# Where the summing transfers of two weight matrices run: moving them from the input projections to the GLA scan and the GLA up-projection

## The chip, the cores and the metric

The kernel runs on one core of one Trainium2 chip. The metric is the device time of one execution in microseconds (us), the median of several runs. A core has a matrix engine (TensorE, in the profile PE, with its weight loads as PEld), three engines for elementwise work (VectorE, in the profile DVE; ScalarE, ACT; GpSimd, POOL) and a queue engine (SyncE, SP). Each engine takes its instructions strictly in order from its own queue, and the five run beside one another, tied together by semaphores. Transfers (DMA) are issued as instructions of an engine's queue and then run on 16 DMA engines that all queues share.

## What is computed

One decoder block on 1024 tokens of width 1024, in float32. Cut to what bears on the change:

```python
proj = n @ w_in                       # split into z, xBC, dt, q, k, v, r, a1, g_ssd, g_gla
y_ssd = ssd_mixer(z, xBC, dt, ...)    # Mamba-2 branch: convolution, then a chunked scan
y_gla = gla_mixer(q, k, v, r, a1, ...)  # gated linear attention: a chunked scan
merged = sigmoid(g_ssd) * (y_ssd @ w_up_ssd) + sigmoid(g_gla) * (y_gla @ w_up_gla)
h = h + merged @ w_o                  # output projection of the mixer
q = rmsnorm(h) @ w_xq                 # query projection of the cross-attention
...                                   # attention over 256 memory tokens, then a SwiGLU FFN
```

## The kernel before

**Products.** Most large products are made by a Strassen scheme: the weight and the activation are cut into quadrants, and seven products of half the size (named B11, B21, T1, B22, T2, T3, T4) replace eight. That needs sums of quadrants. Each operand is then split into a high and a low float32r part, so that three fast passes stand for one float32 product; ScalarE makes the high part (tile `whi`, L233) and VectorE the low part (tile `wlo`, `split`, L228). A `Unit` (L285) makes 256 output columns in seven products of 12 matmuls of 128x512 each; its weight quadrants are in tile `raw`, and the sums of them (`left`, L304) are written to `sa` and `raw` by VectorE or GpSimd. Which of the two is chosen when the program is built: `either` (L85) asks a simple model of how long each of the two is already booked (`Meter`, L58). Everything that is called on GpSimd books time there, the issue of a transfer too, as if it were an elementwise operation over the transfer's whole size. The split weights go into rings of three buffers (L236), so VectorE and ScalarE can run at most some products ahead of TensorE.

**The sums of `w_o` and `w_xq`.** For these two matrices (class `Wide`, L1218) the four quadrant sums aren't made by the engines but by transfers in device memory: `weight_sums` (L482) issues, on GpSimd's queue, copies of quadrants into a buffer (`wos_d` for `w_o`, `xqs_d` for `w_xq`) and further transfers that add a second quadrant on the way (`accum_op`). With the adding ones cut in two halves, a matrix takes 12 transfers. Each is `pinned`: it stands in GpSimd's queue behind everything that was written before it for GpSimd. The FFN's `w_ffn_out` gets the same treatment in pieces (buffer `down_d`, L1821), whose adding transfers are not cut.

**Order of the work.** `run(main, (side, rate), ...)` (L448) walks through a main generator and takes `rate` steps of each side generator after each of its steps. The stages that matter here, in order:

- The z units (L895): 4 units, with `ssd_prep` and `gla_prep` as one side and `wsums`, the 24 summing transfers of both matrices in turn, as another at 0.36 transfers for each product.
- The xBC units (L1052): 6 units, beside them the convolution of the unit before (VectorE, tile `cv`), and again `wsums` at 0.36. Then `drain(wsums)` issues what is left.
- The SSD scan (L1066) beside the units for r, q, k and the first gates.
- The GLA scan (L1191): 5 gate units (35 products) as the main work, and `gla_steps` as the side. Each of the 8 chunks makes, among others, its output on TensorE, squares on ScalarE, a reciprocal root on GpSimd (tile `ss`, L217), a scaling on ScalarE (tile `o`, L1144) and transposes on TensorE (L55).
- The last gate unit, then the SSD up-projection `dense(0, ...)` and the GLA up-projection `dense(1, ...)` (L1366): 16 steps each, of 24 matmuls. A step of the second ends in `post_yg` (L1458): a gate, and then the sum of the two branches into tile `rq`, with the engine chosen by `either`. `wide_side` (L1472) prepares the first operands of the output projection beside it.
- The output projection `wo.steps()`, which reads `wos_d` and the `rq` tiles, then the query projection, which reads `xqs_d`, attention, and the FFN.

A scheduler places each engine's instructions in an order by priority and a model of time when the program is built; on the chip that order is fixed.

Of the kernel before, what the change touches and what calls it, by code (L numbers as in the profile page):

```python
# [16 lines left out]
P = 128  # L17
# [18 lines left out]
PRIO = 1000  # L36
# [42 lines left out]
def block_kernel(ctx: ExitStack, tc: tile.TileContext, t: dict, out: bass.AP):  # L79
# [3 lines left out]
    DVE, POOL = Meter(nc.vector, now, 0.06, 1.04e-3), Meter(nc.gpsimd, now, 0.08, 2.25e-3)  # L83

    def either(ap, slack=0.0):  # L85

        return POOL if POOL.after(ap) - slack < DVE.after(ap) else DVE
# [11 lines left out]
    def dram(name, *shape):  # L99
        return dr.tile(list(shape), F32, name=name, tag=name)  # L100
# [12 lines left out]
    gg_d = dram("gg_d", D, TOK)  # L113
# [4 lines left out]
    wos_d = dram("wos_d", 2 * D, HALF)  # L118
    xqs_d = dram("xqs_d", 2 * D, HALF)
# [10 lines left out]
    add = lambda e, o, a, b: e.tensor_tensor(o, a, b, ALU.add)  # L130
# [3 lines left out]
    pinned = tc.keep_in_program_order  # L134
# [289 lines left out]
    def group(units, B, then=(), nxt=None, frm=6, products=7, order=None):  # L424


        for u in units:
            u.load()
        then = list(then)
        many = len(units)  # L430
        for n, name in enumerate((order or (CHAIN if many > 1 else SPACED))[:products]):
            for x, u in enumerate(units):
                u.step(name, B)
                if many > 1:
                    B.upto((n + 1) * B.kh - (-(x + 1) * B.kh // many))
                if n == 6 and nxt:
                    nxt.upto((x + 1) * nxt.kh // many)
                if n >= frm and then:
                    then.pop(0).load()
                while len(posts) > lag[0]:  # L440
                    settle()
                    if n < 4:
                        break
                yield
        for u in then:
            u.load()

    def run(main, *rest, prio=0):  # L448

        owed = [0.0] * len(rest)  # L450
        for _ in main:
            for i, (g, rate) in enumerate(rest):
                owed[i] += rate
                while owed[i] >= 1.0:
                    owed[i] -= 1.0
                    with tc.high_priority(offset=prio):
                        next(g, None)
# [5 lines left out]
    def drain(g):  # L463
        for _ in g:
            pass

    def singles(units, B, then=()):

        for u, nxt in zip(units, list(units[1:]) + [None]):
            yield from group([u], B, [nxt] if nxt else then)  # L470
# [11 lines left out]
    def weight_sums(todo):  # L482


        jobs = []
        for A, d, n, k0 in todo:
            put = lambda m, d=d, n=n, k0=k0, kn=A.shape[2]: (
                d[(m * n + k0) * P:(m * n + k0 + kn) * P].rearrange("(k p) c -> p k c", p=P))
            q = {(i, j): A[j][:, :, half(i)] for i in range(2) for j in range(2)}
            jobs.append([(put(0), q[1, 0], 0), (put(2), q[0, 0], 0), (put(3), q[0, 1], 0), (put(0), q[1, 1], 1),  # L490
                         (put(2), q[1, 0], 1), (put(1), put(0), 0), (put(1), q[0, 0], 1), (put(3), put(1), 1)])
        for step in zip(*jobs):
            for o, a, more in step:
                kn = o.shape[1]
                for c in (slice(0, kn // 2), slice(kn // 2, kn)) if more and kn > 3 else (slice(0, kn),):
                    if more:
                        pinned(POOL.dma_start(o[:, c], a[:, c], accum_op=ALU.add))
                    else:
                        pinned(POOL.dma_start(o, a))
                    yield  # L500
# [72 lines left out]
    for k in range(NB):  # L573
        p = bank()
# [79 lines left out]
    B = Operands(hb, 4)  # L654
# [232 lines left out]
    xu = [Unit(w_in, 0, XBC0 + 256 * u) for u in XU]  # L887
    zu = w_in_units(Z0, 4, store_rows(sz_d))
    ru = w_in_units(R0, 4, store_rows(sr_d))
    qk = w_in_units(Q0, 2, store_rows(q_d)) + w_in_units(K0, 2, store_rows(k_d))  # L890
    gs = w_in_units(GS0, 4, store_rows(gs_d))
    gg = w_in_units(GG0, 4, store_rows(gg_d))
    prep = chain([ssd_prep(), gla_prep()])
    wsums = weight_sums([(t[w].rearrange("(j k p) c -> j p k c", j=2, p=P), d, 4, 0) for w, d in (("w_o", wos_d), ("w_xq", xqs_d))])
    run(singles(zu, B, xu[:1]), (prep, 1.0), (wsums, 0.36))  # L895
    drain(prep)
    settle_all()
    st2.close()
# [9 lines left out]
    class SSD:  # L908
# [69 lines left out]
        def gate(s):  # L978
            s.y = sp_.tile([P, 4, CH], F32, name="y", tag="y", bufs=3)
            for k in range(4):  # L980
                DVE.scalar_tensor_tensor(s.y[:, k], s.L[:, k], dcol[:, s.g * 4 + k:s.g * 4 + k + 1],
                                         s.py[:, k * P:(k + 1) * P], ALU.mult, ALU.add)
            mul(POOL, s.y, s.y, s.L[:, 4:8])
# [65 lines left out]
    cvp = pool("conv", 1, stack=st2)  # L1049
    pend = iter(())  # L1050
    for n, u in enumerate(XU):
        run(group([xu[n]], B, (xu + ru)[n + 1:n + 2]), (pend, 1.0), (wsums, 0.36))  # L1052
        drain(pend)
        pend = conv(u, xu[n])
        if n == 2:
            it[0].csb = sl_.tile([P, GH, CH], F32, name="xz", tag="xz", bufs=3)
            it[0].fetch_cs()
        if n == 4:
            it[0].load()
    drain(pend)  # L1060
    drain(wsums)
    st2.close()
    sp_ = pool("ssd", 1, stack=st3)
    ssd = ssd_steps()
# [92 lines left out]
    def gla_steps():  # L1157
        it = [GLA(c) for c in range(NCH)]
        it[0].load_qk()
        it[0].load()  # L1160
        it[1].load_qk()
        it[1].load()
        yield
        it[0].decay()
        it[0].start()
        yield
        it[0].attend()
        yield
        for i, a in enumerate(it):
            b = it[i + 1] if i + 1 < len(it) else None  # L1170
            c = it[i + 2] if i + 2 < len(it) else None
            a.out()
            yield
            if c:
                c.load_qk()
            a.scan()
            yield
            if b:
                b.decay()
                b.start()  # L1180
            yield
            a.norm()
            yield
            if b:
                b.attend()
            if c:
                c.load()
            yield

    gla = gla_steps()  # L1190
    run(singles(gs[2:] + gg[:3], B, gg[3:]), (gla, 8 * 5 / 30), prio=PRIO)  # L1191
    drain(gla)
    st4.close()
    st_early.close()

# [4 lines left out]
    ysg_d = dram("ysg_d", D, TOK)  # L1200
# [9 lines left out]
    def quad(src, base, i, j):  # L1210
        q = rp.tile([P, HALF], F32, name="ga", tag="ga")
        SP.dma_start(q, src[base + i * P:base + (i + 1) * P, half(j)])
        return q
# [152 lines left out]
    def dense(no, ins, post, pre=lambda o, j: None, js=JS, left=left):  # L1366

        todo = [(o, j) for o in range(NB) for j in (js if o + 1 < NB else js[::-1])]
        got = [pre(*x) for x in todo[:2]]
        for n, (o, j) in enumerate(todo):  # L1370
            w = left[NB * no + o]
            if n + 2 < len(todo):
                got.append(pre(*todo[n + 2]))
            cur = got[n]
            p = acc()
            m = 0
            for k in range(NB):
                for a, b in ((0, 0), (0, 1), (1, 0)):
                    PE.matmul(p, w[:, a, k], ins[k][:, b, half(j)], start=m == 0, stop=m == 3 * NB - 1)
                    m += 1  # L1380
            with ahead():
                post(o, j, p, cur)
            yield

    EVEN, ODD = ("op",) * 8, ("op",) * 6 + ("aux",) * 2
    i_ys, i_yg, i_q, i_xo = (paired(x) for x in (EVEN, ODD, EVEN, EVEN))
# [71 lines left out]
    def post_yg(o, j, p, gy):  # L1458
        g, y = gy
        gated(g, p)  # L1460
        q = wo.quad(o // 4, j)[:, o % 4]
        add(either(g), q, g, y)

    def post_wo(i, j, u, q):
        o = 4 * i + u
# [4 lines left out]
    wo = Wide(t["w_o"], wos_d, post_wo, ("aux",) * 7, ("m", "m", "m", "aux"), xT_d, 0.5)  # L1470

    def wide_side(x, n, m, pin=None):  # L1472
        for _ in range(n):
            yield
        x.load(1)
        for _ in range(m):
            yield
        x.load(2)
        yield
        x.prep(1, pin)  # L1480
        yield
        x.prep(2, pin)
        yield
# [18 lines left out]
            yield  # L1502

    run(dense(0, i_ys, post_ys, lambda o, j: gate(gs_d, o, j)), (fetch_gated(yg_d, sr_d, i_yg), 1.0))
    run(dense(1, i_yg, post_yg, lambda o, j: (gate(gg_d, o, j), quad(ysg_d, o * P, 0, j))), (wide_side(wo, 8, 4, pinned), 1.0))
    run(wo.steps(), (wide_side(xq, 7, 2), 1.0))


# [128 lines left out]
    for u in range(D_FF // 256):  # L1637
# [5 lines left out]
        gate = Unit(t["w_ffn_in"], 0, 256 * u, post=gpost, key="aux")  # L1643
# [38 lines left out]
    B = Operands(b_xo, 4, order=("B11", "T1", "B21", "B22", "T2", "T3", "T4"))  # L1682
# [139 lines left out]
    for u in range(1, len(gu)):  # L1822
        gate, up = gu[u]
# [78 lines left out]
```

## Time and profile before

| What | Value |
|---|---|
| Median of 3 runs | 1950.2 us (1948.35 to 1950.63) |
| The profiled execution's own time | 1951.16 us |
| Its span, first to last instruction | 1949.5 us |
| TensorE busy | 1901.7 us, 98% of the span |
| VectorE busy | 1352.9 us, 69% |
| ScalarE busy | 880.5 us, 45% |
| GpSimd busy | 509.4 us, 26% |
| Mean granted TensorE clock | 0.995 |
| Moved by GpSimd's transfers | 39.85 MB, 9.7% of the 16 DMA engines' time |

The page of the profile has the busy shares in 40 slices of the span (a digit is tenths). The view of windows gives, for stretches of the span, each engine's busy time with the number of its instructions, the granted TensorE clock, the DMA engines' mean busy share and the rate moved. TensorE's busy time alone says little, since matmuls overlap and their ends are modelled; the number of matmuls that a stretch holds says more. The view of waits gives, for each pair of a waiting group and its releaser, the sum, the number and the longest of the waits; "issue" as a releaser stands for a wait whose cause the profile doesn't name. The timeline gives start, duration, engine, line, operation, output and inputs, and in brackets the idle time of the engine before it.

### The profile page before, as it was taken

How to read it: one execution, taken by the hardware profiler on the slowest of the kernel's cores; microseconds unless marked ns; L12 is line 12 of the kernel's file. 1: busy time of each engine (PE TensorE's matmuls, PEld its weight loads, DVE VectorE, ACT ScalarE, POOL GpSimd, SP SyncE). 2: the span in 40 equal slices, each digit the busy share in tenths (PEclk: the TensorE clock that was granted, in tenths of full speed). 3: DMA queues.
4: the chain of work that ended last, by engine and by line, in shares of the span. 5: the costliest groups of instructions: out<-in, count | busy, mean ns of one | idle time of the engine just before them, and what ended most of it. 6: DMA issues, size and time to landing. Idle time of an engine off the chain costs nothing.

```text
span 1949.5 us, 26093 instructions
## 1 busy us (share of the span) xinstructions
PE 1901.7 (98%) x9680; PEld 1598.3 (82%) x9680; DVE 1352.9 (69%) x1949; ACT 880.5 (45%) x1521; POOL 509.4 (26%) x412
## 2 busy tenths in 40 slices
PE   7999989899999999999999999999999999999998
PEld 7998767778878888888888888888888888888888
DVE  7765858677767755553377786677878877766566
ACT  7534445455554344553235564543333333345243
POOL 0112444354544222000002100006444544330002
PEclk9999999999999999999999999999999999999999
DMA  9425698654654554595444430434665657387463
GB/s 345 139 93 187 194 282 249 151 184 152 186 179 137 193 157 153 210 374 172 140 151 157 157 98 12 146 103 128 172 180 149 166 154 191 87 298 267 158 225 122
DMA packets 242915, 341.04 MB, mean 175 GB/s; under 512 B 16458, under 2 KB 147764, under 8 KB 242788
## 3 DMA queue, kind: packets, MB, share of 16 engines
q1 hardware_dynamic: 225572, 293.23, 44.7%
q0 software_dynamic: 15488, 39.85, 9.7%
q10 hardware_dynamic: 1728, 6.29, 0.8%
q8 instruction: 76, 1.25, 0.3%
q14 instruction: 51, 0.42, 0.1%
HBM read 249.87 MB, written 129.30 MB: 195 GB/s over the span
## 4 chain that ended last, share of the span: by engine, by line
PE 84%; DVE 7%; issue 4%; POOL 2%; DMA 2%; ACT 1%; SPq 0%; POOLq 0%; DVEq 0%; ACTq 0%
PE acc L51 68%; PE bank L51 15%; PE bank L55 2%; DVE cv L73 2%; DVE wlo L73 2%; DVE hs L73 1%; DVE o L73 1%; DMA hl<-ys_d 0%; DMA down_d<-in_w_ffn_out_dram 0%; POOL ssum L73 0%; POOL raw L73 0%; DVE gx L73 0%; DMA raw<-in_w_ffn_in_dram 0%; DVE gy L73 0%; ACT cv L778 0%
## 5 line engine op out<-in xcount | busy, mean ns | idle before, releaser
L73 DVE TENSOR_TENSOR wlo<-raw,whi 128x512 fp32r<-128x512 f32 x272 | 237.6, 880 | 114.2 <-ACT whi L233 111.8
L233 ACT ACTIVATE whi<-raw 128x512 fp32r<-128x512 f32 x272 | 169.8, 631 | 260.6 <-PE acc L51 201.2
L51 PE MATMUL acc<-hl,wd 128*128 128x512 f32 x1152 | 263.8, 390 | 1.9 <-ACT wd L233 1.4
L51 PEld LDWEIGHTS acc<-hl,wd 128*128 128x128 f32 x1152 | 215.5, 188 | 48.5 <-ACT wd L233 2.6
L73 DVE TENSOR_TENSOR o<-acc,o 128x512 f32<-128x512 f32 x244 | 167.2, 685 | 89.6 <-PE acc L51 85.8
L51 PE MATMUL acc<-fs 128*128 128x512 f32 (+1 forms) x792 | 155.7, 355 | 0.1
L51 PEld LDWEIGHTS acc<-fs 128*128 128x128 f32 x792 | 130.7, 189 | 20.8 <-issue 0.5
L73 DVE TENSOR_TENSOR fs<-fr,fs 128x1024 fp32r<-128x1024 f32 (+1 forms) x78 | 93.0, 1226 | 36.7 <-ACT fs L233 36.5
L233 ACT ACTIVATE fs<-fr 128x1024 fp32r<-128x1024 f32 (+1 forms) x78 | 74.3, 984 | 93.7 <-PE acc L51 29.7
L73 POOL TENSOR_TENSOR ssum<-ssum,sq 128x512 f32<-128x512 f32 (+1 forms) x17 | 29.5, 1733 | 322.4 <-ACT sq L519 308.8
L233 ACT ACTIVATE whi<-sa 128x512 fp32r<-128x512 f32 x96 | 59.6, 627 | 102.5 <-PE acc L51 85.7
L73 POOL TENSOR_TENSOR sa<-raw 128x512 f32<-128x512 f32 x42 | 62.7, 1494 | 134.8 <-DMA raw<-in_w_in_dram 65.9
L73 DVE TENSOR_TENSOR wlo<-sa,whi 128x512 fp32r<-128x512 f32 x96 | 75.5, 787 | 23.9 <-ACT whi L233 23.0
L51 PE MATMUL acc<-ws 128*128 128x512 f32 x384 | 88.8, 389 | 0.0
L51 PEld LDWEIGHTS acc<-ws 128*128 128x128 f32 x384 | 72.0, 188 | 14.9
L73 POOL TENSOR_TENSOR raw<-raw,sa 128x512 f32<-128x512 f32 x34 | 47.8, 1406 | 138.0 <-DVE wlo L73 138.0
L51 PE MATMUL acc<-B22h,whi 128*128 128x512 f32 x192 | 76.9, 400 | 6.1 <-ACT whi L233 5.8
L51 PE MATMUL acc<-T2h,whi 128*128 128x512 f32 x192 | 76.8, 400 | 5.7 <-ACT whi L233 5.7
L51 PE MATMUL acc<-T4h,whi 128*128 128x512 f32 x192 | 76.4, 398 | 3.6 <-DVE o L73 3.5
L51 PE MATMUL acc<-B22h,wlo 128*128 128x512 f32 x192 | 76.6, 399 | 1.8 <-DVE wlo L73 1.7
L51 PE MATMUL acc<-T3h,wlo 128*128 128x512 f32 x192 | 75.4, 393 | 1.5 <-DVE wlo L73 1.5
L51 PE MATMUL acc<-T1h,whi 128*128 128x512 f32 x192 | 76.4, 398 | 0.1
(420 smaller groups left out, 4995.7 us busy)
## 6 DMA issues: line engine op xcount, KB each, us to landing
raw<-in_w_in_dram SPq DMA_DIRECT2D x26, 1024.0 KB, 7.1
raw<-in_w_ffn_in_dram SPq DMA_DIRECT2D x22, 1024.0 KB, 8.8
act_d<-o SPq DMA_DIRECT2D x77, 256.0 KB, 2.7
fr<-act_d SPq DMA_DIRECT2D x35, 512.0 KB, 5.4
down_d<-in_w_ffn_out_dram POOLq DMA_DIRECT2D x18, 768.0 KB, 7.3
fr<-down_d SPq DMA_DIRECT2D x20, 512.0 KB, 4.2
ga<-h_d SPq DMA_DIRECT2D x32, 256.0 KB, 6.8
csb<-cs_d SPq DMA_DIRECT2D x15, 512.0 KB, 3.9
```

Source lines behind the costliest of these rows:

```text
L51: return s.e.matmul(o, x, y, **kw)
L55: return s.e.transpose(o, x, i)
L73: return f(*a, **kw)
L233: pin(ACT.activation(hi, src, AF.Copy))
```

## The change

It does four things.

1. The summing transfers leave the z and xBC stages. Those of `w_o` now run beside the GLA scan, at 0.37 transfers for each product and at the scan's own raised priority, and what is left of them is issued after it; those of `w_xq` run beside the GLA up-projection, at 0.8 for each step.
2. The two matrices are no longer taken in turn: each has a sequence of its own.
3. The order within a sequence changes. It was: copy 0, copy 2, copy 3, add to 0, add to 2, copy 0 to 1, add to 1, add 1 to 3. Now copy 3 stands between "copy 0 to 1" and "add to 1". This holds for the FFN's pieces too.
4. The sum of the branches in `post_yg` always goes to GpSimd.

```diff
@@ weight_sums
-            jobs.append([(put(0), q[1, 0], 0), (put(2), q[0, 0], 0), (put(3), q[0, 1], 0), (put(0), q[1, 1], 1),
-                         (put(2), q[1, 0], 1), (put(1), put(0), 0), (put(1), q[0, 0], 1), (put(3), put(1), 1)])
+            jobs.append([(put(0), q[1, 0], 0), (put(2), q[0, 0], 0), (put(0), q[1, 1], 1), (put(2), q[1, 0], 1),
+                         (put(1), put(0), 0), (put(3), q[0, 1], 0), (put(1), q[0, 0], 1), (put(3), put(1), 1)])
@@ z units
-    wsums = weight_sums([(t[w].rearrange("(j k p) c -> j p k c", j=2, p=P), d, 4, 0) for w, d in (("w_o", wos_d), ("w_xq", xqs_d))])
-    run(singles(zu, B, xu[:1]), (prep, 1.0), (wsums, 0.36))
+    run(singles(zu, B, xu[:1]), (prep, 1.0))
@@ xBC units
-        run(group([xu[n]], B, (xu + ru)[n + 1:n + 2]), (pend, 1.0), (wsums, 0.36))
+        run(group([xu[n]], B, (xu + ru)[n + 1:n + 2]), (pend, 1.0))
...
     drain(pend)
-    drain(wsums)
@@ GLA scan
+    def dense_sums(w, d):
+        return weight_sums([(t[w].rearrange("(j k p) c -> j p k c", j=2, p=P), d, 4, 0)])
+
     gla = gla_steps()
-    run(singles(gs[2:] + gg[:3], B, gg[3:]), (gla, 8 * 5 / 30), prio=PRIO)
+    wsums = dense_sums("w_o", wos_d)
+    run(singles(gs[2:] + gg[:3], B, gg[3:]), (gla, 8 * 5 / 30), (wsums, 0.37), prio=PRIO)
     drain(gla)
+    drain(wsums)
@@ post_yg
-        add(either(g), q, g, y)
+        add(POOL, q, g, y)
@@ GLA up-projection
-    run(dense(1, i_yg, post_yg, lambda o, j: (gate(gg_d, o, j), quad(ysg_d, o * P, 0, j))), (wide_side(wo, 8, 4, pinned), 1.0))
+    wsums = dense_sums("w_xq", xqs_d)
+    run(dense(1, i_yg, post_yg, lambda o, j: (gate(gg_d, o, j), quad(ysg_d, o * P, 0, j))), (wide_side(wo, 8, 4, pinned), 1.0), (wsums, 0.8))
+    drain(wsums)
```

## The prediction

> **What bounds the kernel now.** I read the page first, for what is busy; then windows of 25 us, for where TensorE does less than it can; then the waits and GpSimd's timeline in those windows, for who is late.
>
> ```profile
> span 1949.5 us, 26093 instructions
> PE   7999989899999999999999999999999999999998
> ```
>
> TensorE is busy nearly everywhere, so what is not TensorE's own work can save little. Where it falls behind, the count of matmuls shows:
>
> ```profile
> core 0: us, PE busy (x) PEld busy (x) DVE busy (x) ACT busy (x) POOL busy (x), PEclk, DMA share, GB/s
> ...
> 200.00:225.00 25.00, 22.58 (x98) 17.82 (x97) 20.80 (x19) 12.99 (x18) 10.78 (x11) 1.00 0.62 177
> 225.00:250.00 25.00, 24.66 (x108) 19.79 (x107) 20.79 (x26) 8.58 (x16) 7.60 (x11) 1.00 0.71 192
> 250.00:275.00 25.00, 19.18 (x74) 15.21 (x73) 7.79 (x10) 9.31 (x12) 9.98 (x9) 0.86 0.98 263
> 275.00:300.00 25.00, 24.27 (x104) 18.91 (x102) 19.04 (x23) 15.61 (x21) 9.50 (x7) 1.00 1.06 349
> 300.00:325.00 25.00, 22.89 (x97) 18.00 (x98) 24.29 (x25) 11.98 (x17) 11.17 (x7) 1.00 0.82 262
> 325.00:350.00 25.00, 24.87 (x109) 19.90 (x107) 24.29 (x22) 12.72 (x17) 15.46 (x12) 1.00 0.65 158
> 350.00:375.00 25.00, 24.55 (x108) 20.36 (x109) 18.26 (x23) 10.50 (x14) 4.48 (x4) 1.00 0.81 216
> 375.00:400.00 25.00, 18.55 (x74) 13.65 (x73) 16.53 (x15) 9.34 (x13) 12.30 (x8) 0.86 0.30 74
> ...
> 1325.00:1350.00 25.00, 25.00 (x112) 20.71 (x111) 16.68 (x19) 8.33 (x14) 20.09 (x15) 1.00 0.37 117
> ```
>
> A window without gaps holds 112 of these matmuls (last row), so one costs 25 / 112 = 0.223 us. In the z and xBC stages every window is short, and two hold only 74, with the clock at 0.86. Their waits:
>
> ```profile
> ACT whi L233 <- POOL raw L73: 12.8, 1, 12.8
> PE acc L51 <- ACT whi L233: 5.8, 1, 5.8
> ```
>
> ```profile
> ACT whi L233 <- POOL sa L73: 12.4, 1, 12.4
> PE acc L51 <- ACT whi L233: 5.4, 1, 5.4
> ```
>
> In 250 to 275 TensorE waited 5.8 us for a split weight, ScalarE 12.8 us for a sum from GpSimd; from 370 on it was 5.4 and 12.4 us. Why GpSimd was late, its timeline tells:
>
> ```profile
> 252.67 1.16 POOL L73 DMA_DIRECT2D xqs_d<-in_w_xq_dram  x1 [5.37 <-issue]
> ...
> 262.14 1.14 POOL L73 DMA_DIRECT2D wos_d<-in_w_o_dram  x1 [7.30 <-issue]
> 262.88 1.70 POOL L73 TENSOR_TENSOR raw<-raw,sa 128x512 f32<-128x512 f32 x1
> ```
>
> ```profile
> 369.19 1.14 POOL L73 DMA_DIRECT2D xqs_d<-xqs_d  x1 [4.92 <-issue]
> 378.39 1.15 POOL L73 DMA_DIRECT2D xqs_d<-xqs_d  x1 [8.06 <-issue]
> 379.10 1.73 POOL L73 TENSOR_TENSOR sa<-raw 128x512 f32<-128x512 f32 x1
> ```
>
> Each late sum stands behind summing transfers at which GpSimd's queue was held 5 to 8 us. That is about a landing:
>
> ```profile
> DMA to landing us min/median/max: 5.3/6.3/9.0
> ...
> DMA to landing us min/median/max: 5.4/7.3/11.5
> ```
>
> (first `wos_d`, then `xqs_d`). I read it so: a summing transfer is issued only once the one before has landed, even when it belongs to the other matrix. The stage offers them too fast for that:
>
> ```profile
> L73 POOL DMA_DIRECT2D xqs_d<-in_w_xq_dram x9: 754/1142/1169, 165.8 to 343.4; - x9
> ...
> L73 POOL DMA_DIRECT2D xqs_d<-xqs_d x3: 777/1142/1153, 307.8 to 378.4; - x3
> ```
>
> 24 transfers (12 of each matrix) from 165.8 to 378.4 are one in 9.2 us; their landing and GpSimd's own work between fill that, and the queue is nearly always held.
>
> **Part 1: what leaves the z and xBC stages.** With the 24 transfers go the two stalls. The first window's neighbours hold 108 and 104, mean 106; the second's neighbour before it 108. Missing: 32 + 34 = 66 matmuls, 14.7 us. Bounds: the waits alone, 5.8 + 5.4 = 11.2; up to full windows, 2 x 38 x 0.223 = 16.9. I take 14.7, since the neighbours have this stage's other troubles. Next in line after a stall is VectorE (20.8 to 24.3 of 25 us busy in the short windows), not GpSimd: the other six windows miss 48 matmuls, 10.7 us, and most of that stays. I credit 1.0 us (0 to 10.7). Sums that `either` now sends to GpSimd instead of VectorE ride in that credit.
>
> The clock is part of these 14.7 us: 0.86 over 25 us is 3.5 us of lost clock at each stall. [...]
>
> **Part 2: `w_o` beside the GLA scan.**
>
> ```profile
> 640.00:808.00 168.00, 168.00 (x828) 142.89 (x827) 96.03 (x199) 76.59 (x186) 39.33 (x33) 1.00 0.50 159
> 912.00:1000.00 88.00, 88.00 (x390) 72.85 (x389) 37.54 (x46) 19.04 (x22) 0.00 (x0) 1.00 0.38 126
> 1000.00:1025.00 25.00, 25.00 (x112) 20.71 (x111) 25.00 (x27) 11.85 (x12) 0.00 (x0) 1.00 0.58 210
> 1300.00:1760.00 460.00, 459.93 (x2044) 380.53 (x2043) 362.51 (x446) 170.53 (x278) 208.48 (x147) 1.00 0.60 171
> ```
>
> 35 products in 168 us, at 0.37: one transfer in 13.0 us, against a median landing of 6.3. Issue (1.2 us x 12) fits into GpSimd's 128 idle us. A hold comes only where two transfers stand together in its queue; behind it wait unit sums and a chunk's root:
>
> ```profile
> 717.35 1.02 POOL L73 TENSOR_TENSOR ss<-ss,mhalf 128x4 f32<-128x4 f32 x1 [3.85 <-DVE ss L73]
> 718.40 1.57 ACT L1144 ACTIVATE o<-bank,ss 128x256 f32<-128x256 f32 x4 [1.41 <-POOL ss L73]
> 721.37 0.27 PE L55 MATMUL bank<-ident,o 128*128 128x128 f32 x1
> ```
>
> From the scaled output (719.97) to its transposes are 1.4 us of slack. A hold of 4.92 us (the shortest above) in front of a root costs 4.92 - 1.4 = 3.5 us. I take one such hold, at even odds: 1.8 us. Bounds: nothing, or all 8 chunks, 28. The transfers do not stand in SP's queue with the stage's loads, but share the DMA engines with them. These were 0.50 busy here; in the stage that the transfers leave they were 0.62 to 1.06 busy from 200 to 350, and neither of the two stalls there was put down to a late load. I add nothing. If sums go to VectorE because GpSimd is booked by transfers, it has 72 idle us to take them.
>
> **Part 3: `w_xq` beside the up-projection, and the forced sum.** 16 steps in 88 us, at 0.8: one transfer in 6.9 us, about a landing, so GpSimd will be held for much of the stage. But nothing ran there (0.00), and the new tenants are the 16 sums alone.
>
> ```profile
> L73 DVE TENSOR_TENSOR rq<-gates,ga 128x512 f32<-128x512 f32 x5 | 3.5, 690 | 0.1
> ```
>
> ```profile
> L73 POOL TENSOR_TENSOR sa<-raw 128x512 f32<-128x512 f32 x42 | 62.7, 1494 | 134.8 <-DMA raw<-in_w_in_dram 65.9
> ```
>
> ```profile
> 1004.97 0.69 DVE L73 TENSOR_TENSOR rq<-gates,ga 128x512 f32<-128x512 f32 x1
> 1005.57 1.22 DVE L73 TENSOR_TENSOR rq<-rq 128x1024 f32<-128x1024 f32 x1
> ```
>
> A sum moves from 0.69 us on VectorE to about 1.49 on GpSimd. The early ones are read steps of 5.5 us (88 / 16) later. The last is followed at once by a combination on VectorE, which has no idle time from 1000 to 1025: 1.49 - 0.69 = 0.8 us later. I charge 0.8; bounds: nothing, since 11 us leave VectorE, or a hold of 4.92 besides, 5.7. The readers of the finished sums are far off:
>
> ```profile
> L1249 SPq DMA_DIRECT2D wr<-wos_d x4: 360/372/1470, 980.3 to 1002.2; - x4
> ```
>
> ```profile
> L1249 SPq DMA_DIRECT2D wr<-xqs_d x4: 374/438/1827, 1055.0 to 1085.8; - x4
> ```
>
> `wos_d` is read 172 us after the scan ends at 808, `xqs_d` 55 us after the up-projection ends at 1000: covered.
>
> [...]
>
> **Part 4: the order within a sequence, in the FFN.**
>
> ```profile
> POOL down_d L73 <- DMA down_d<-in_w_ffn_out_dram: 24.6, 4, 7.5
> ```
>
> GpSimd waits up to 7.5 us there today, and TensorE loses 0.07 of 460 us (the last of the four windows). A copy between the dependent transfers can shorten these waits, worth at most 0.07; a hold moved to another place is most likely covered like the present ones. Zero, with one uncovered hold of 3.5 us as the bad end.
>
> **Sum.** -14.7 - 1.0 + 1.8 + 0.8 + 0 = -13.1 us. The profiled execution took 1951.16 us (span 1949.5 and 1.7 around it), 1.0 above the median of 1950.2. It would take 1938.1; the median 1937.1, rounded 1937.
>
> **The rivals.**
> - *Slower: the holds move into the scan.* The raised priority packs transfers together, and they stand in front of the roots. For it: roots and unit sums share the queue, with 1.4 us of slack. Against: 13.0 us between transfers. All 8 chunks at 3.5 us in place of Part 2's 1.8: 1937 + 28 - 1.8 = 1963. It turns slower from the fifth held chunk on (5 x 3.5 - 1.8 = 15.7, more than 13.1). Chance 0.12.
> - *No change: two stalls like the removed ones come back,* in the scan or where the up-projection's transfers make loads late (the DMA share, 0.38, could rise towards the 0.98 and 1.06 of the z stage). 1937 + 14.7 = 1952. For it: GpSimd held for most of that stage. Against: no TensorE wait there, and no late consumer but the last sums. Chance 0.08.
> - *Faster still: the short windows fill up,* because VectorE's delays too came from GpSimd and full DMA engines. 1937 - (16.9 - 14.7) - (10.7 - 1.0) = 1925. Against: VectorE at 24.29 of 25 us. Chance 0.10.
>
> **How the numbers follow.** My forecast has 0.70. About 0.2% (3.9 us) is what a measurement of this kernel can tell from no change: 1946.3 to 1954.1. Faster: 0.68 of the forecast, all of the last rival, and 0.03 of the first, for a scan with few holds: 0.81. Same: 0.02 of the forecast and 0.05 of the second rival: 0.07. Slower: 0.09 of the first and 0.03 of the second: 0.12. The range runs from 1928, which leaves out the far end of the filled windows, to 1949, where the forecast carries the held up-projection and two more held chunks (1937 + 4.9 + 7); most of the two slow cases lies beyond.
>
> **What would show it.** Right: no window of the z and xBC stages at clock 0.86, 100 or more matmuls in each, no wait of ScalarE above 10 us on `raw` or `sa`; GpSimd, which is idle between 912 and 1000 today, busy there with the 16 sums; TensorE without gaps in the scan. Part 2 is wrong if transposes of `o` wait on ScalarE and ScalarE on `ss`; Part 3 if VectorE waits for `rq`. The forecast falls if GpSimd was late for another reason, and windows of 74 matmuls stay.

## The result and the profile after

| | before | after |
|---|---|---|
| Median | 1949.28 us (1947.68 to 1950.63, 4 runs) | 1938.1 us (1937.67 to 1939.03, 4 runs) |
| Profiled execution | 1951.16 us | 1939.03 us |

The ratio is 0.9944, 95% interval 0.9926 to 0.9961: faster by 0.6%. The forecast was 1937. The total is right; the two largest terms behind it are not, as the stages show.

The page of after, its span and TensorE's slices:

```profile
span 1937.3 us, 26098 instructions
...
PE   7999999999999999899999999999999999999998
```

The 8s of before near the start are gone, and a new one stands in the 17th slice, at about 800 us. The windows of after, columns as in the prediction:

```profile
250.00:275.00 25.00, 25.00 (x112) 20.68 (x111) 16.74 (x19) 16.19 (x21) 6.65 (x5) 1.00 0.99 353
275.00:300.00 25.00, 24.09 (x105) 19.25 (x105) 23.64 (x25) 14.65 (x20) 11.68 (x7) 1.00 0.58 220
...
375.00:400.00 25.00, 24.42 (x134) 19.91 (x134) 18.74 (x27) 20.83 (x44) 10.31 (x8) 1.00 0.58 189
```

Neither window of 74 matmuls is left: they hold 112 and 134, at a clock of 1.00 (from 380 on the matmuls are partly smaller ones, so 134 is no measure of gaps), and of the short neighbours the next one holds 105. TensorE's waits from 200 to 425 are down to these:

```profile
PE acc L51 <- DVE o L73: 2.0, 2, 1.5
PE acc L51 <- DVE wlo L73: 1.6, 5, 0.9
```

Further on time is given back. First before, then after, the same two windows at the end of the GLA scan and the start of the SSD up-projection:

```profile
750.00:775.00 25.00, 25.00 (x123) 21.24 (x122) 14.34 (x37) 11.62 (x31) 4.01 (x3) 1.00 0.48 159
...
800.00:825.00 25.00, 24.03 (x112) 19.88 (x111) 14.24 (x20) 16.06 (x28) 2.30 (x2) 1.00 0.78 280
```

```profile
750.00:775.00 25.00, 23.02 (x105) 19.37 (x105) 16.11 (x32) 9.92 (x25) 9.80 (x8) 0.93 0.66 157
...
800.00:825.00 25.00, 18.97 (x68) 14.56 (x68) 11.66 (x14) 15.54 (x22) 0.00 (x0) 0.80 1.04 374
```

To see what each stage gained, I set the start of the n-th matmul in the trace of before against that of the n-th matmul in the other trace; both have 9680. The difference is the lead so far. Steps of 200 matmuls are coarse, and each row is one execution (those of after, e5, e6b, e11 and e14 are among the longest of their kernel, those of e7 and e10 the shortest), but the sums close: after's last lead, 12.1, is 1951.16 - 1939.03.

| lead in us at | n = 1400 (z units) | 2200 (xBC done) | 3600 (GLA scan) | 4400 (end of scan) | 4600 (SSD up-projection) | 9600 (end) |
|---|---|---|---|---|---|---|
| after | -1.1 | 22.3 | 24.2 | 20.5 | 12.5 | 12.1 |
| e1_dense0 | -2.0 | 21.5 | 23.6 | 23.8 | 18.1 | 17.9 |
| e2_store_act | -0.5 | 23.6 | 24.0 | 20.2 | 14.3 | 14.0 |
| e3_either | -1.4 | 22.9 | 23.9 (n = 3400) | 17.4 | 14.2 | 13.4 |
| e5_booked | -1.1 | 23.3 | 24.8 | 20.9 | 12.7 | 12.4 |
| e6_traffic | -25.1 | -1.7 | 0.8 | -3.1 | -11.6 | -11.9 |
| e6b_traffic | -1.3 | 22.1 | 21.9 | 16.7 | 9.6 | 8.8 |
| e7_xq_only | 0.2 | 16.1 | 17.2 | 17.3 | 17.6 | 18.0 |
| e10_hold | -1.5 | 25.9 | 25.9 | 23.8 | 15.7 | 13.2 |
| e11_before_dve | 0.2 | 6.1 | 6.6 | 6.2 | 6.3 | 5.8 |
| e12_after_dve | 0.1 | 27.5 | 29.8 | 23.5 | 15.4 | 12.7 |
| e14_unbooked | -0.6 | 22.9 | 24.1 | 16.8 | 8.5 | 8.0 |
| e17_marker | -0.8 | 26.5 | 28.1 | 28.1 | 28.0 | 24.5 |

After gains 23.4 us in the z and xBC stages, where 15.7 were forecast, and 1.9 in the SSD scan; it loses 3.7 in the GLA scan and 8.0 at the boundary behind it, where 1.8 was forecast; the rest costs 0.4.

What was late in the scan: waits of after from 740 to 762, then SyncE's timeline, then GpSimd's.

```profile
POOL sa L73 <- DMA raw<-in_w_in_dram: 9.8, 1, 9.8
DVE qk L73 <- DMA qk<-q_d: 6.3, 1, 6.3
...
ACT o L1142 <- POOL ss L73: 5.1, 1, 5.1
```

```profile
741.41 0.39 SPq L299 DMA_DIRECT2D raw<-in_w_in_dram  x1
742.10 1.73 SPq L1087 DMA_DIRECT2D qk<-q_d  x1
```

```profile
739.09 1.17 POOL L73 DMA_DIRECT2D wos_d<-in_w_o_dram  x1 [5.89 <-DMA wos_d<-wos_d]
750.09 1.29 POOL L73 TENSOR_TENSOR sa<-raw 128x512 f32<-128x512 f32 x1 [9.83 <-DMA raw<-in_w_in_dram]
...
754.88 1.04 POOL L73 TENSOR_TENSOR ss<-ss,mhalf 128x4 f32<-128x4 f32 x1
```

A root (`ss`) is late and ScalarE waits 5.1 us for it, as the prediction feared; but no held transfer stands right in front of it. GpSimd waited for the raw weights' load, VectorE for `q`, and both loads were issued 2 to 3 us after a summing transfer. The last chunk's `q` load has 8.50 us on after's chain. In before, by SyncE's and VectorE's timelines, it is issued at 762.38 and in use 2.8 us later. First after, then before:

```profile
742.10 8.50 DMA qk<-q_d
```

```profile
762.38 0.37 SPq L1089 DMA_DIRECT2D qk<-q_d  x1
```

```profile
765.21 0.69 DVE L73 SCALAR_TENSOR_TENSOR qk<-qk,e 128x512 f32<-128x512 f32 x1 [2.46 <-DMA qk<-q_d]
```

At the boundary no hold takes part at all. The chain that ended last in after, in order of time:

```profile
798.99 10.98 DMA yg_d<-qk
...
810.05 1.06 ACT wd L233
```

The last chunk's store takes 10.98 us to land (the one at 739.15 has 2.94 on the same chain), ScalarE's split of the up-projection's next weights waits for it, and TensorE runs dry. The granted clock in the window is 0.80, up to 0.20 x 25 = 5.0 us of lost clock.

Something else changed at this place: the plan. Matched by name in the order of start, 644 of the 756 matmuls from n = 3684 to 4439 stand elsewhere than in before, in after and in every kernel below with `w_o`'s transfers beside the scan; e1, e7, e11 and e17 have before's order there. The scan's last transpose comes 29 matmuls ahead of the up-projection's first one, where it was 50. So the last store is later in part by plan.

The GLA up-projection, beside which the `w_xq` transfers now run, and the FFN:

```profile
912.00:1000.00 88.00, 88.00 (x390) 72.88 (x389) 41.18 (x35) 20.66 (x24) 31.55 (x27) 1.00 0.83 237
...
1300.00:1760.00 460.00, 459.45 (x2035) 380.20 (x2034) 354.40 (x431) 171.14 (x272) 207.43 (x147) 1.00 0.61 174
```

TensorE has no gap while the `w_xq` transfers run (DMA share 0.83, from 0.38), and loses 0.55 us instead of 0.07 in the FFN.

### The profile page after: what moved, and what is told of

The parts are those of the page before. It is cut to its first block, busy times and chain, and to the rows that moved or that the text cites. A ratio compares the mean times of both kernels' runs of the same rounds, so it can differ in the third digit from the quotient of the medians.

```text
span 1937.3 us, 26098 instructions
## 1 busy us (share of the span) xinstructions
PE 1898.9 (98%) x9680; PEld 1600.8 (83%) x9680; DVE 1359.5 (70%) x1935; ACT 882.1 (46%) x1521; POOL 533.6 (28%) x426
## 4 chain that ended last, share of the span: by engine, by line
PE 85%; DVE 7%; DMA 3%; issue 2%; ACT 1%; POOL 1%; SPq 0%; POOLq 0%; DVEq 0%; ACTq 0%
PE acc L51 69%; PE bank L51 14%; DVE cv L73 2%; PE bank L55 2%; DVE wlo L73 2%; DVE o L73 1%; DVE hs L73 1%; DMA yg_d<-qk 1%; DMA hl<-ys_d 0%; DMA qk<-q_d 0%; DMA raw<-in_w_ffn_in_dram 0%; DMA down_d<-in_w_ffn_out_dram 0%; POOL ssum L73 0%; ACT cv L778 0%; DVE gy L73 0%
## 5 line engine op out<-in xcount | busy, mean ns | idle before, releaser
L73 DVE TENSOR_TENSOR wlo<-raw,whi 128x512 fp32r<-128x512 f32 x272 | 243.6, 903 | 97.3 <-ACT whi L233 97.3
L73 POOL TENSOR_TENSOR sa<-raw 128x512 f32<-128x512 f32 x42 | 68.3, 1625 | 149.2 <-DMA raw<-in_w_in_dram 80.3
L51 PEld LDWEIGHTS acc<-ws 128*128 128x128 f32 x384 | 71.9, 188 | 15.2 <-DVE ws L73 0.3
L51 PE MATMUL acc<-T3h,whi 128*128 128x512 f32 x192 | 75.7, 394 | 2.0 <-DVE o L73 2.0
L73 POOL TENSOR_TENSOR rstd<-rstd,mhalf 128x4 f32<-128x4 f32 (+1 forms) x7 | 8.7, 1250 | 247.8 <-DVE rstd L73 247.8
```

The lines of the kernel that those rows point to most:

```text
L51: return s.e.matmul(o, x, y, **kw)
L73: return f(*a, **kw)
```

## The experiments

Every time stands beside the kernel before on the same chip, at 1947.5 to 1948.1 us. Intervals are those of the ratio.

**e1_dense0: the `w_o` transfers beside the SSD up-projection, none beside the scan.**

```diff
-    run(singles(gs[2:] + gg[:3], B, gg[3:]), (gla, 8 * 5 / 30), (wsums, 0.37), prio=PRIO)
+    run(singles(gs[2:] + gg[:3], B, gg[3:]), (gla, 8 * 5 / 30), prio=PRIO)
...
+    wsums = dense_sums("w_o", wos_d)
+    run(dense(0, i_ys, post_ys, lambda o, j: gate(gs_d, o, j)), (fetch_gated(yg_d, sr_d, i_yg), 1.0), (waiting(wsums, 4), 1.0))
```

> The summing transfers of w_o run beside the SSD up-projection (from its fifth step on) instead of beside the GLA scan; all else as in the changed kernel. Between the start of the scan and the first step of the SSD up-projection the changed kernel gave back 11.7 us of its lead over the kernel before (24.2 us ahead, then 12.5). Theory: the transfers beside the scan cost this (late loads of q and k, held roots, a late last store). Then the lead stays near 24 us and the time is 1926 to 1929. Rival: the scan itself, started earlier and ordered anew, loses it without any transfer beside it: 1936 to 1940. If the transfers now stall the up-projection, TensorE waits between 800 and 900 us would show it.

1932.79 us, ratio 0.9923 (0.9909 to 0.9936): some 4 us better than after by the two ratios (0.9944), whose intervals overlap a little; it lies between the theory's time and the rival's. The scan keeps the whole lead (23.6 to 23.8); the boundary still loses 5.7. The transfers weren't held back as written: nothing in GpSimd's queue kept them, and they began at 784.9, among the loads of the up-projection's first operand. GpSimd's timeline, the chain, and a window of this kernel:

```profile
784.90 0.98 POOL L73 DMA_DIRECT2D wos_d<-in_w_o_dram  x1
```

```profile
788.93 13.78 DMA hl<-ys_d
```

```profile
800.00:825.00 25.00, 20.12 (x80) 16.45 (x81) 10.06 (x10) 11.35 (x14) 3.51 (x3) 0.86 1.07 356
```

The load on the chain takes 13.78 us; two others of this operand, whose landing the trace gives, took 7.1 and 8.3. With after, that makes two places of the transfers and two late loads.

**e2_store_act: the last chunk's store on ScalarE's queue.** It asks whether the store was late by SyncE's queue.

```diff
-            SP.dma_start(yg_d[:, s.tk].rearrange("(k p) s -> p k s", p=P), s.qk)
+            (ACT if s.c == NCH - 1 else SP).dma_start(yg_d[:, s.tk].rearrange("(k p) s -> p k s", p=P), s.qk)
```

> The changed kernel, but the GLA scan's last store (yg_d, chunk 7) is issued from ScalarE's queue instead of SyncE's. In the changed kernel it took 11.0 us to land, queued behind the loads for the up-projection, and ScalarE's second weight split for the up-projection waited for it while TensorE lost some 8 us with the clock. Theory: a queue of its own brings the store down in 3 to 5 us and most of that stall goes: 1930 to 1934. Rival: the store is late because the scan is late, and its landing is slow because all 16 DMA engines are full: 1937 or more.

1937.18 us, 0.9951 (0.9938 to 0.9964): no change that can be told, as the rival had it. The store still has 9.37 us on the chain. The boundary loses 5.9 instead of 8.0, but e3, whose store is as in after, loses 3.2, so the difference can't be put down to the queue. SyncE's queue isn't what makes the store late.

**e5_booked: the plan books GpSimd as if the 24 transfers were still in z/xBC.** With nothing to issue, `either` still shares the sums as it did before: three of those in z/xBC go to VectorE, as in before, where after has none. (At this rate 22 of the 24 bookings fall due.)

```diff
+    def booked():
+        for w in (2048, 2048, 2048, 2048, 2048, 2048) + (1024,) * 8 + (2048, 2048) + (1024,) * 8:
+            POOL.t = max(POOL.t, now[0]) + POOL.fixed + POOL.each * w
+            yield
```

> The changed kernel, with GpSimd booked in the model that chooses the engine (not on the chip) in the z and xBC stages as if the 24 transfers were still issued there; no instruction is added. The matmul counts show that these two stages gained 23.4 us, where 14.7 + 1.0 were forecast. Theory: what was gained is that GpSimd's queue is no longer held, the choice of engines gives little: 1937 to 1940. Rival: the choice of engines (more sums on GpSimd, fewer on VectorE) gave the 8 us that were not forecast: 1945 or more.

1937.44 us, 0.9945 (0.993 to 0.9961), lead 23.3 after xBC. The gain doesn't come from another share of the sums.

**e6_traffic and e6b_traffic: after, with plain 1 MB copies in z/xBC.** The copies serve no purpose; 16 MB is what the two matrices' transfers write (8 steps of 1 MB each). Sixteen copies were meant, but at their rate only 12 fell due, in both kernels. In the first kernel nothing fixed their place, in the second each is pinned in SyncE's order.

```diff
+            o = dram(f"dummy{n}", HALF, HALF)
+            pinned(SP.dma_start(o, w[half(n // 2 % 2), half(n // 4 % 2)]))
```

> The changed kernel with 16 plain copies of 1 MB between buffers in device memory, issued from SyncE's queue at an even rate in the z and xBC stages: as many bytes (16 MB) as the summing transfers wrote there, without holding GpSimd. Theory (held queue): 1937 to 1942. Rival (the transfers' traffic on the 16 DMA engines delayed loads, stores and the convolution): the 8 us that were not forecast come back, 1945 or more, and with them the counts of 97 to 104 matmuls in 25 us.

> After with sixteen plain 1 MB copies between DRAM tensors, issued from SyncE one by one through the z/xBC stages; the copies serve no purpose. Theory (held queue of GpSimd): without a hold, traffic costs the z/xBC stages little; lead at their end 18 to 23 us, 1937 to 1943 us. Rival (traffic of the transfers, which delays the loads there): at least half of the lead is lost, 1948 us or more.

The first took 1963.21 us, 1.0078 (1.0064 to 1.0092), and tells nothing of z/xBC: its copies were placed at the kernel's start, where the lead is already -25.1 at n = 1400, and z/xBC gained its 23.4 as in after. The second took 1940.11 us, 0.9952 (0.9936 to 0.9968), with a lead of 22.1 after xBC, the theory's. Its copies, and the window in which they raise the DMA share most: 0.97, where after has 0.58 and before had 1.06.

```profile
L898 SPq DMA_DIRECT2D dummy<-in_w_xq_dram x6: 496/497/3542, 173.9 to 274.9; - x6
L898 SPq DMA_DIRECT2D dummy<-in_w_o_dram x6: 496/786/2769, 180.1 to 293.7; - x6
```

```profile
275.00:300.00 25.00, 24.75 (x108) 19.87 (x107) 21.52 (x25) 15.61 (x21) 6.52 (x6) 1.00 0.97 364
```

12 MB, copied plainly from SyncE, cost TensorE almost nothing there. That is fewer bytes than the transfers wrote, and none of them fall on the time of the second stall, 375 to 400.

**e7_xq_only: `w_o`'s transfers back in z/xBC, one in about 17 us; `w_xq`'s as in after.**

```diff
-    run(singles(zu, B, xu[:1]), (prep, 1.0))
+    run(singles(zu, B, xu[:1]), (prep, 1.0), (wsums, 0.18))
```

> As after, but w_o's twelve transfers go back into the z/xBC stages, one per about 17 us; w_xq's stay beside the up-projection, and the scan and the boundary have none. Theory (a hold of GpSimd hurts only while the next transfer is queued behind one that has not landed, and the transfers in the scan are what delayed its q and k loads and the last chunk's store): with 17 us between transfers that land in 6 to 8 us, the z/xBC stages keep 18 to 23 us of the lead, nothing is lost in the scan and at most 4 us at the boundary: 1926 to 1931 us. Rival (the presence of accumulating transfers in z/xBC is what cost the 23 us, by their traffic): half of them back takes about half of it back, 10 to 12 us, and the scan's and boundary's loss of 11 goes: 1934 to 1940 us.

1936.5 us (1933.35 to 1938.23, 5 runs), 0.9935 (0.9922 to 0.9949); the profile is of the shortest. The theory's time was missed and the rival's met: z/xBC keeps 16.1 instead of 22.3, a loss of 6.2 where the rival had 10 to 12. The other four runs took 2.7 to 4.9 us more than the traced one; where isn't known. GpSimd is held only twice between 200 and 400, 8.31 and 4.70 us. A z row's load is on the chain for 19 us, the first 7.8 of them in being issued:

```profile
247.40 19.18 DMA zr<-sz_d
```

But scan and boundary lose nothing (17.2, 17.3, 17.6). The window that had 68 matmuls in after:

```profile
800.00:825.00 25.00, 23.94 (x104) 19.07 (x104) 14.28 (x15) 17.76 (x22) 0.00 (x0) 1.00 1.05 397
```

From the scan on, the text of this kernel differs from after's only in that `w_o`'s transfers are gone, and TensorE's order is again that of before. So the 11.7 us that after loses there come from placing them there, by the late loads or by the order that came with them.

**e10_hold and e14_unbooked: after, with bursts of sixteen fills on GpSimd in z/xBC.** A burst keeps GpSimd busy (a fill took 0.366 us at the mean in e10, sixteen of them 5.9) and moves nothing between memories; 22 of the 24 bursts fell due. In the second kernel (`nc.gpsimd.memset`) the fills bypass the planner's booking, so that sums still go to GpSimd.

```diff
+    def holds():
+        for _ in range(24):
+            for _ in range(16):
+                pinned(POOL.memset(idle_t, 0.0))
+            yield
```

> After with 24 bursts of sixteen fills of a small tile on GpSimd, spread through the z/xBC stages: each burst occupies GpSimd for about 5 us and moves no data between memories. Theory (what cost the time was GpSimd's queue held while its sums waited): most of the 23 us is lost again, 1950 to 1965 us. Rival (the transfers' traffic or their use of the DMA queues): the bursts cost little, 1937 to 1942 us.

> As the run with bursts of fills, but the plan that shares sums between VectorE and GpSimd does not know of the bursts, as it does not know of a transfer's hold: so the raw sums queue behind the bursts on GpSimd, with no transfer in z/xBC. Theory (a sum queued behind a hold is what costs): of the lead of 23 to 26 us at the end of xBC 8 us or more is lost, 1945 us or more. Rival (holds do not matter, something else about the transfers does): the lead stays above 20 us, 1941 us or less.

The first took 1940.04 us, 0.9957 (0.994 to 0.9973); the second 1941.74 us, 0.9967 (0.9954 to 0.998). Leads after xBC: 25.9 and 22.9. In both my theory failed. In the first, `either` had moved all raw sums to VectorE, so nothing stood behind the bursts: a window has 109 matmuls with VectorE at 23.1 us. In the second sums do stand among the bursts, GpSimd is busy for 23 of 25 us, ScalarE waits up to 5.5 us for a sum, and TensorE barely notices. One window of each:

```profile
275.00:300.00 25.00, 24.89 (x109) 20.12 (x109) 23.09 (x32) 14.41 (x21) 21.61 (x60) 1.00 0.56 218
```

```profile
275.00:300.00 25.00, 25.00 (x112) 20.67 (x111) 22.95 (x24) 14.62 (x20) 23.20 (x45) 1.00 0.58 215
```

One reservation: the scheduler knows how long a fill takes and orders the sums around it; it can't know how long a transfer is held. The bursts show that a busy GpSimd is no harm by itself, not that an unforeseen hold is none.

**e3_either: the query-up's twelve sums (the change's fourth part) free again.**

```diff
-        add(POOL, q, g, y)
+        add(either(g), q, g, y)
```

> After with the query-up's twelve sums free again to go to VectorE or GpSimd, by their planned finish, in place of GpSimd alone. My step put the fixed choice at 0 to 0.5 us: 1937 to 1939 us. Rival (the choice matters: sums forced behind transfers on GpSimd come late, or VectorE's sums delay its weight expansions): a difference of 2 us or more to either side.

1937.79 us, 0.9945 (0.9932 to 0.9959): the same as after. (The stage's sums are sixteen; "query-up" is the GLA up-projection.)

**e11_before_dve and e12_after_dve: the raw sums of the z and xBC units on VectorE always,** once in the kernel before, once in after.

```diff
+    for u in zu + xu:
+        u.e = DVE
```

> The kernel before, all transfers where they were in z/xBC, with one edit: the sums of the raw weight blocks of the z and xBC units go to VectorE always, so that none can queue behind a transfer on GpSimd. Theory (the two stalls were sums of TensorE's next weights, queued on GpSimd behind a transfer that waited for the one ahead of it; neither the hold itself nor the transfers' traffic costs TensorE anything): the z/xBC stages gain 20 to 26 us over before, and scan and boundary lose nothing, as there is nothing new in them: 1922 to 1928 us, faster than after. Rival 1 (the traffic of the transfers delays the raw loads there): half or less of it, 1936 us or more. Rival 2 (VectorE has no room for these sums): no gain, 1945 us or more.

> After with the same edit: the z and xBC units' raw sums on VectorE always, with no transfer in these stages. It is the control of the kernel before with that edit. Theory: the lead at the end of xBC is 23 to 26 us, equal within 3 us to that of the kernel before with the edit; the scan and the boundary lose their 11 to 12 us as in after: 1934 to 1938 us. Rival (the transfers' traffic): this kernel's lead at the end of xBC is more than 5 us larger than that of the kernel before with the edit.

Before with this edit: 1938.44 us, 0.9955 (0.9941 to 0.9968). Its six runs fall into two groups, four at 1937.2 to 1939.0 and two at 1945.4; the trace is of one at 1945.4, so it shows the worse group, and the lead of the other isn't known stage by stage. After with it: 1938.59 us, 0.995 (0.9938 to 0.9961), lead 27.5 after xBC. So VectorE has room for the sums, and the transfers still cost the traced run 27.5 - 6.1 = 21.4 us. The theory fell, the rival of late loads stands. From n = 1400 to 1600, on to 2000 and on to 2200 this run gains 5.5, 1.2 and -0.8 us, where its control gains 11.4, 6.0 and 10.0: about half of what is missing is missing at the second stall. Two things are late in that trace. The first, by ScalarE's and SyncE's timelines:

```profile
261.17 0.63 ACT L233 ACTIVATE whi<-raw 128x512 fp32r<-128x512 f32 x1 [1.59 <-DMA raw<-in_w_in_dram]
```

```profile
247.54 0.55 SPq L299 DMA_DIRECT2D raw<-in_w_in_dram  x1
```

ScalarE splits the raw weights 13.6 us after their load was issued. The landing of this load (the one issued at 246 to 251) in before, then in after:

```profile
DMA to landing us min/median/max: 13.3/13.3/13.3
```

```profile
DMA to landing us min/median/max: 9.7/9.7/9.7
```

It is 13.5 in e11 and 15.2 in e7, where transfers run, and 9.6 to 10.6 in e10, e12 and e14, where none do. In e6b, between two plain copies, ScalarE waited for the load until 10.6 us after its issue. So the load was late in before too, and its lateness goes with the transfers. The second, by the waits from 340 to 400 and GpSimd's timeline, is the sum of the first R unit, whose engine I hadn't fixed:

```profile
ACT whi L233 <- POOL sa L73: 13.2, 1, 13.2
```

```profile
371.06 1.15 POOL L73 DMA_DIRECT2D xqs_d<-xqs_d  x1 [8.06 <-issue]
371.77 1.73 POOL L73 TENSOR_TENSOR sa<-raw 128x512 f32<-128x512 f32 x1
```

That is the prediction's own picture, a sum behind the last transfers, and here it costs a stall. In e7, where the last transfer is issued at 361.9 instead of 378.4, the lead grows by 9.1 us from n = 2000 to 2200, in after by 9.9.

**e17_marker: a version that beats both.** As e1, with the sums of z, xBC and the GLA up-projection on VectorE, and a small copy on GpSimd that reads the up-projection's first product, so that the transfers behind it can't start while that stage's loads are under way.

```diff
+        if (o, j) == (0, 0):
+            pinned(POOL.tensor_copy(mark, g[:, :8]))
```

> A version meant to keep all of the gain. No transfer in z/xBC or beside the scan; w_o's twelve stand on GpSimd behind a small copy that reads the first product of the SSD up-projection, so that none can start while that stage's y loads are still under way; w_xq's twelve follow them. The raw sums of the z and xBC units and the query-up's sums are on VectorE. Theory (what the change lost beside the scan and at the start of the up-projection is lateness of loads that shared the DMA engines with transfers): the lead at the end of xBC is 25 to 28 us and nearly all of it is kept through the scan and the boundary: 1919 to 1926 us. Rival (VectorE's sums, or GpSimd's backlog of 24 transfers, come back as a wait by the output projection): 1930 us or more.

1926.73 us (1925.69 to 1927.61, 4 runs), 0.9889 (0.9872 to 0.9905): faster than before by 1.1%, though just outside the theory's range. The lead is 28.1 in the scan and 28.0 behind the boundary: nothing is lost there. Its marker, its first transfers, and the window that had 68 matmuls in after and 80 in e1:

```profile
811.96 0.19 POOL L73 COPY mark<-gates 128x8 f32<-128x8 f32 x1 [31.33 <-DVE gates L73]
812.09 0.98 POOL L73 DMA_DIRECT2D wos_d<-in_w_o_dram  x1
821.89 0.78 POOL L73 DMA_DIRECT2D wos_d<-in_w_o_dram  x1 [8.82 <-issue]
```

```profile
800.00:825.00 25.00, 25.00 (x112) 20.70 (x111) 12.89 (x17) 15.10 (x23) 1.89 (x3) 1.00 1.05 400
```

The DMA engines are as full as in e1 (1.05 and 1.07); what differs is that the loads that are needed next are already in (the eight of the up-projection's first operand were issued from 777.8 to 790.3, with 7.4 to 7.7 us to landing where the trace gives it). The 3 us between the theory's lead and the end go in the FFN (27.7 at n = 8000, 24.7 at 8200); why wasn't followed.

## Why the prediction came out right, point by point

**The total** is right by luck, by two errors that cancel. In the terms of the rivals, "faster still" and "two stalls come back" both came true in part, each given a small chance alone.

**Part 1 (-15.7; measured -23.4).** The mechanism's first link is right: the stalls of 250 and 375 went with the transfers, and ScalarE's longest wait for `raw` or `sa` there is 2.3 us. The size was off twice. Over the matmuls that before starts in the two windows the lead grows by 8.7 and 9.5 us, 18.2 together instead of 14.7 and above the bound of 16.9. I measured the stalls against neighbours that the transfers had themselves made short, and in the second window I counted shorter matmuls as if they were of the full size. And the rest of the two stages, whose short windows I credited with 1.0 of their 10.7 since VectorE seemed the limit, gave the remaining 5.2. At 112 matmuls VectorE is busy for 22.95 us (e14), at 97 it was 24.29: so high a share was no proof of a limit.

**The cause in Part 1** is only partly what I wrote. The second stall fits it: in e11 the sum still stands behind the last transfers and the stall stays; in e7 and e12 no transfer stands in front of it, and it goes. In the first stall the sum was the last wait, but the load of the next weights was late as well: 13.3 us to landing, 13.5 and 15.2 in the other two kernels with transfers there, 9.6 to 10.6 in those without. Moving the sums (e11) brought back 5.5 of 11.4 us there, in a trace of its longer runs, and spacing the transfers (e7) still left 6 us lost with late loads. A busy GpSimd (e10, e14) and the share of the sums (e5) cost nothing like it. Plain copies didn't either (e6b), but of 12 MB instead of 16. Which property of the summing transfers makes loads late stays open: adding in memory, GpSimd's queue, the bytes that they read to add, or when they are issued. Plain copies from GpSimd's queue, and adding ones from elsewhere, weren't tried.

**Part 2 (+1.8; measured +11.7).** The step that failed is "I add nothing" for the DMA engines that the transfers share with the scan's loads. I had argued that neither stall of before was put down to a late load; that was the last waiter, not the only one. Loads and the last store were late, within the scan (8.5 us for a `q` load) and past its end (10.98 us for the store), where I had placed no cost at all. e1 (transfers among the loads, 5.7 us lost) and e17 (transfers behind the loads, nothing lost) show it for the boundary, with one order of TensorE in both. For after's own 11.7 us the order that the plan gave the scan changed too, and no kernel has that order without the transfers; how the loss divides between late loads and order isn't known. A part of it is clock: e3, with after's order and a wait of 3.2 us at the boundary, but the clock at 1.00, lost 3.2 us there instead of 8.0 (and 6.5 in the scan). Nor were the transfers 13.0 us apart: the first five started 8 to 9 us apart, each when the one ahead had landed. The hold in front of a root, my own term, was not seen to cost.

**Part 3 (+0.8; measured 0.2) and Part 4 (0; measured 0.3)** lie inside their bounds. That the choice of engine costs nothing, e3 confirms.

## What to carry to other kernels

In this kernel a background transfer had two prices: what waited in its queue (ScalarE for 13.2 us on a sum in e11), and the loads that were late beside it (a raw load took 13.3 us to land in before, 9.7 in after); the row of a wait named only the last of the two, and when e11 took the first stall's sums away the late load stayed. Look for the next loads on which the path depends, and start background transfers by a data dependence behind them, not by a rate (in e17 the lead behind the boundary was 28.0 us, in after 12.5). Judge a stall's size against windows without the suspect, not against neighbours that share it.

## What the runs showed of the hardware

**After a wait of 2.0 us the clock was 0.52, and after one of 3.2 us it was 1.00.** After's TensorE timeline has a gap of 1.98 us, for VectorE's `o`; behind it windows of 2 us:

```profile
755.53 0.39 PE L51 MATMUL acc<-B21h,wlo 128*128 128x512 f32 x1
757.89 0.61 PE L51 MATMUL acc<-T3h,whi 128*128 128x512 f32 x1 [1.98 <-DVE o L73]
```

```profile
756.00:758.00 2.00, 0.10 (x1) 0.14 (x2) 2.00 (x7) 2.00 (x6) 0.73 (x1) 1.00 0.36 41
758.00:760.00 2.00, 2.00 (x8) 1.69 (x9) 2.00 (x7) 1.05 (x3) 0.00 (x0) 0.52 0.88 360
760.00:762.00 2.00, 2.00 (x14) 2.00 (x13) 1.46 (x3) 0.60 (x1) 0.46 (x1) 0.63 0.67 256
```

The clock was 0.52 and 0.63 over the next 4 us: 2 x 0.48 + 2 x 0.37 = 1.7 us lost on top of the wait. So this gap cost more than its own length (matmul ends are modelled; from start to start it was 757.89 - 755.53 = 2.36 us). The length alone doesn't tell these waits apart. At the boundary TensorE waited 3.7 us in after, and the clock fell (0.80 in that window); in e3 it waited 3.2 us there, and the clock stayed at 1.00:

```profile
800.00:825.00 25.00, 20.57 (x88) 15.97 (x87) 13.26 (x14) 14.47 (x19) 2.38 (x2) 1.00 1.07 358
```

That is 88 matmuls, where after has 68.

**A VectorE operation took 3.18 us instead of 1.21 beside a sum on GpSimd.** The forced sums on GpSimd met VectorE operations with two inputs. In after, one group of these with its least, median and longest time, then one such pair on VectorE's and GpSimd's timelines:

```profile
L73 DVE TENSOR_TENSOR ws<-rq,ws x6: 1207/1212/3181, 977.9 to 1005.5; 128x1024 fp32r<-128x1024 f32 x6
```

```profile
987.03 3.18 DVE L73 TENSOR_TENSOR ws<-rq,ws 128x1024 fp32r<-128x1024 f32 x1
```

```profile
987.40 1.72 POOL L73 TENSOR_TENSOR rq<-gates,ga 128x512 f32<-128x512 f32 x1
```

The operation takes 1.21 us at the median; beside the sum it took 3.18, longer by 1.97 where GpSimd's own lasted 1.72. It is no single case: of VectorE's `wlo<-raw,whi` of 128x512 in after, whose inputs are the loaded weights and ScalarE's high part, the 178 that meet no GpSimd tensor operation take at most 0.70 us, and 72 of the 88 that share more than 0.2 us with one take over 0.9. `o<-acc,o`, one input of which is `acc`, the accumulator that the matmuls write, takes at most 0.69 us either way. Why the one grows and the other doesn't isn't shown. Under the up-projection the longer times were covered: TensorE is busy for 88.00 of the 88 us from 912 to 1000.

**The summing transfers ran one at a time.** In e17, where nothing else is in GpSimd's queue, the second starts 9.8 us after the first (821.89 - 812.09), held for 8.82 of it. The landing of that kernel's `wos_d` transfers:

```profile
DMA to landing us min/median/max: 5.3/9.3/10.2
```

The second starts 0.3 us after the first has landed (812.09 + 9.5), and in all the traces no transfer of the two matrices starts before the one ahead of it has landed (in before and after each starts at least 0.26 us later). Whether the chip or the program's own semaphores see to that isn't shown. The hold is about a landing, as the prediction read it from before. It is longer here than there (median 9.3 against 6.3 us), in a stage whose DMA share is 1.05.
